# Double-size loads for the first two thirds of a load-bound kernel, and fifteen small loads among the last pieces

**The chip, the cores, the metric.** One core of a Trainium2 chip. The metric is the device time of one execution in microseconds (us). Profiled runs give a span a little shorter than the time (325.4 us for 327.0). PE, ACT, DVE, POOL and SP are the core's tensor, scalar, vector, GpSimd and sync engines; the sixteen transfer engines move data between memory and the core.

## The reference

```python
B, S, D, H = 8, 2048, 2048, 8          # x: (B, S, D) fp32, 134.2 MB; bias: (H, D // H)
x_heads = x.reshape(B, S, H, D // H).transpose(0, 2, 1, 3) + bias[None, :, None, :]
x_tiled = np.repeat(x_heads, 2, axis=2)
mx = x_tiled.max(axis=-1, keepdims=True)
lse = mx.squeeze(-1) + np.log(np.exp(x_tiled - mx).sum(axis=-1))      # (8, 8, 4096)
```

Every element of x is read once; 1 MB is written. The work is exp, a sum over 256 columns, and a logarithm.

## The kernel before

x goes through in 64 tiles of 2 MB: 128 partitions, two rows of 8 KB each. Loads are issued by SP. From tile 57 on a tile comes in two pieces of 1 MB, and tile 63 in eight smaller ones, so that the work after the last byte is short. Within a tile the bias is added, or its exp multiplied in, on PE, POOL and DVE, exp is ACT's, and DVE sums.

```python
K = 2                  # rows of x per partition in a tile
NBUF = 9               # tile buffers
STAGES = [(0, (BULK,)), (54, (MIXED,)), (57, (PROMPT_F1, PROMPT_F1)), (62, ...), (63, ...)]

xts = [sb.tile([P, K, D], F32, name=f"xt{i}") for i in range(NBUF)]

def rows_of(t):
    b, blk = divmod(t, NBLK)
    v = x[b, blk * P * K : (blk + 1) * P * K, :]
    if b < B - 1:
        return v.rearrange("(p k) d -> p k d", k=K)      # 16 KB in one piece per partition
    return v.rearrange("(k p) d -> p k d", k=K)          # tiles 56 to 63: rows of 8 KB

def load(t):
    after = last_uses[t - NBUF] if t >= NBUF else []
    for k0, k1, c0, c1 in pieces(t):
        loads[t, k0, c0] = on_x(t, nc.sync.dma_start(
            out=xts[t % NBUF][:, k0:k1, c0:c1], in_=rows_of(t)[:, k0:k1, c0:c1]), after)
...
# at the end of tile t's work
if k1 == K and t + NBUF < T:
    load(t + NBUF)
```

The softmax here doesn't subtract the row's maximum and nothing guards it: scores larger than these inputs give would overflow.

## Time and profile before

| | before |
|---|---|
| time, median (2 runs) | 326.97 us (326.91 to 327.03) |
| span of the profiled run | 325.4 us |
| read, rate over the span | 134.23 MB, 416 GB/s |
| busiest engines | POOL 290.7 us (89%), DVE 284.0 (87%) |

The transfer engines are busy throughout, and POOL and PE wait for loads (20.1 and 23.1 us in all), ACT and DVE mostly for them; the prediction shows the lines. Two views are added here. The first is the busy time of each engine in two stretches (from:to, its length, then busy time and number of instructions of PE, PE's weight loads, DVE, ACT and POOL; last come PE's granted clock, the busy share of the transfer engines and GB/s).

```profile
15.00:205.00 190.00, 158.96 (x371) 57.13 (x371) 172.96 (x78) 158.84 (x243) 176.61 (x39) 0.94 1.01 428
285.00:310.00 25.00, 23.91 (x87) 11.23 (x87) 24.66 (x120) 24.06 (x50) 19.08 (x35) 0.88 1.01 421
```

The last number of each line: 428 GB/s with 16 KB rows, 421 in the tail with 8 KB rows.

The second is the times at which the sixteen transfer engines report a load as landed. A load has landed when the last of the sixteen has reported (ACT takes up tile 62's second piece at 314.65, the sixteenth report came at 314.63). Taken from the trace (us):

```
load                        first engine   last engine   apart
tile 0                          7.61           8.51       0.90
tile 41                       208.63         210.31       1.68
tile 55                       277.14         279.52       2.38
tile 56 (first of 8 KB rows)  282.11         284.48       2.37
tile 62, second piece         311.91         314.63       2.72
last piece of tile 63         317.27         319.78       2.51
```

The engines drift apart, from 0.90 us to 2.51, and don't come together again. The last one sets when a piece can be used, and the program ends 5.6 us after its last report.

### The profile page before, as it was taken

What the parts mean: (1) busy time and instruction counts of PE and PEld (TensorE: products, weight loads), DVE (VectorE), ACT (ScalarE), POOL (GpSimd) and SP (SyncE); (2) the same over time, 40 slices, a digit from 0 to 9 for tenths busy, and PEclk for the clock granted to TensorE, in tenths of its full rate; (3) what the DMA queues carried; (4) which work ended last, traced back from release to release, by engine and by line L of the source; (5) the groups of instructions that cost most, each with busy time, mean ns of one, the idle gap of its engine ahead of it and who ended that gap; (6) DMA issues with size and microseconds to landing.
All of it is one profiled execution on the core that took longest, in us unless ns stands there. A gap on an engine that the chain in (4) does not pass through costs nothing.

```text
span 325.4 us, 2350 instructions
## 1 busy us (share of the span) xinstructions
PE 263.2 (81%) x649; PEld 98.6 (30%) x649; DVE 284.0 (87%) x306; ACT 264.7 (81%) x425; POOL 290.7 (89%) x123
## 2 busy tenths in 40 slices
PE   5398999599888789779779788887877897399984
PEld 2033333233323223223223223323223332044442
DVE  1008999999999999998998899989899799999985
ACT  1139999499969878987887969698788778889995
POOL 7999999899999999999999999999999899958874
PEclk9999999899979987997997979798998989569999
DMA  7999999999999999999999999999999999999995
GB/s 293 428 435 429 427 433 422 425 433 429 427 427 431 425 424 433 425 425 434 426 425 431 431 422 427 429 429 427 431 427 426 429 425 429 415 421 421 424 394 154
DMA packets 11934, 135.42 MB, mean 416 GB/s; under 512 B 1361, under 2 KB 1745, under 8 KB 2961
## 3 DMA queue, kind: packets, MB, share of 16 engines
q1 hardware_dynamic: 11824, 135.27, 98.9%
q8 instruction: 5, 0.08, 0.1%
q14 instruction: 7, 0.06, 0.0%
q0 software_dynamic: 96, 0.00, 0.0%
q10 hardware_dynamic: 2, 0.01, 0.0%
HBM read 134.23 MB, written 1.05 MB: 416 GB/s over the span
## 4 chain that ended last, share of the span: by engine, by line
DMA 48%; DVE 35%; POOL 6%; ACT 6%; PE 3%; issue 1%; SPq 0%; DVEq 0%
DMA xt<-in_x_dram 45%; DVE R L350 29%; ACT xt L331 5%; DVE xt L343 5%; POOL xt L325 4%; DMA b<-bparts 2%; PE pair L275 2%; DVE xt L366 2%; PE one_ps L275 1%; ACT xt L293 1%; DMA brow<-in_bias_dram 1%; POOL brest L173 1%; POOL brest L175 1%; PE pair L216 0%; POOL bparts L172 0%
## 5 line engine op out<-in xcount | busy, mean ns | idle before, releaser
L325 POOL TENSOR_TENSOR xt<-xt,b_rep 128x2048 f32<-128x2048 f32 x57 | 258.8, 4543 | 20.1 <-DMA xt<-in_x_dram 20.1
L350 DVE TENSOR_REDUCE R<-xt 128x14 f32<-128x3584 f32 (+1 forms) x56 | 214.5, 3831 | 1.9
L331 ACT ACTIVATE xt<-xt 128x2560 f32<-128x2560 f32 (+5 forms) x77 | 158.1, 2062 | 13.4 <-POOL xt L325 12.5
L275 PE MATMUL pair<-xt,ident 128*128 128x512 f32 x216 | 115.1, 660 | 0.0
L275 PE MATMUL one_ps<-xt,ident 128*128 128x512 f32 x108 | 66.7, 702 | 23.1 <-DMA xt<-in_x_dram 23.1
L293 ACT ACTIVATE xt<-pair 128x1024 f32<-128x1024 f32 x54 | 56.3, 1042 | 20.7 <-PE pair L275 19.3
L275 PEld LDWEIGHTS pair<-xt,ident 128*128 128x128 f32 x216 | 46.2, 214 | 61.5 <-issue 61.5
L343 DVE TENSOR_TENSOR xt<-xt,w_ps 128x512 f32<-128x512 f32 x54 | 36.8, 681 | 27.8 <-ACT xt L331 27.7
L286 ACT ACTIVATE xt<-one_ps 128x256 f32<-128x256 f32 x108 | 40.6, 391 | 7.9 <-PE one_ps L275 7.9
L216 PE MATMUL one_ps<-b,ones 3*128 3x512 bf16 x54 | 20.7, 383 | 18.4 <-ACT xt L286 12.4
L216 PEld LDWEIGHTS <-ones 3*128 3x128 bf16 x162 | 13.5, 92 | 70.2 <-issue 63.8
L216 PE MATMUL pair<-b,ones 3*128 3x512 bf16 x108 | 32.3, 378 | 0.0
L275 PEld LDWEIGHTS one_ps<-xt,ident 128*128 128x128 f32 x108 | 17.0, 198 | 46.4 <-DMA xt<-in_x_dram 39.6
L251 PE MATMUL pair<-xt,ident 128*128 128x512 f32 (+1 forms) x36 | 21.0, 669 | 7.2 <-DMA xt<-in_x_dram 7.1
L286 ACT ACTIVATION_READ_ACCUMULATOR xt<-one_ps 128x1 f32 x108 | 23.5, 218 | 0.0
L366 DVE CUSTOM_DVE_ANT_0 xt<-xt,w_ps 128x256 f32<-128x256 f32 x61 | 22.4, 419 | 0.0
L390 POOL TENSOR_TENSOR xt<-xt 128x128 f32<-128x128 f32 (+3 forms) x39 | 13.9, 356 | 3.1
L382 POOL TENSOR_TENSOR xt<-xt,w_sb 128x256 f32<-128x256 f32 (+1 forms) x13 | 10.1, 773 | 5.4 <-ACT xt L331 4.8
L266 PE MATMUL tpair<-ident 128*128 128x128 f32 x84 | 13.6, 300 | 0.5 <-ACT res L421 0.5
L306 ACT ACTIVATE xt<-pair 128x256 f32<-128x256 f32 x33 | 12.3, 387 | 0.0
L266 PEld LDWEIGHTS tpair<-ident 128*128 128x128 f32 x84 | 11.1, 200 | 4.1 <-issue 3.0
L366 DVE CUSTOM_DVE_ANT_0 xt<-xt,one_ps 128x256 f32<-128x256 f32 x27 | 10.6, 416 | 0.7 <-ACT xt L331 0.7
(40 smaller groups left out, 68.5 us busy)
## 6 DMA issues: line engine op xcount, KB each, us to landing
xt<-in_x_dram SPq DMA_DIRECT2D x57, 2048.0 KB, 30.8
xt<-in_x_dram SPq DMA_DIRECT2D x12, 1024.0 KB, 24.7
xt<-in_x_dram SPq DMA_DIRECT2D x4, 256.0 KB, 11.4
out_dram<-res SPq DMA_DIRECT2D x1, 896.0 KB, 6.6
xt<-in_x_dram SPq DMA_DIRECT2D x2, 384.0 KB, 16.0
xt<-in_x_dram SPq DMA_DIRECT2D x2, 128.0 KB, 6.3
out_dram<-res_last SPq DMA_DIRECT2D x1, 128.0 KB, 1.7
b<-bparts POOLq DMA_DIRECT2D x3, 1.5 KB, 6.4
```

Source lines behind the costliest of these rows:

```text
L216: nc.tensor.matmul(p, lhsT=ones3, rhs=each_row(b3, h * Dh, Dh, K), start=True, stop=False,)
L251: mm = nc.tensor.matmul(p, lhsT=ident, rhs=xts[t % NBUF][:, ka:kb, c : c + w], start=False, stop=True,)
L266: nc.tensor.matmul(tps[B % 2][:, 0], lhsT=ident, rhs=ident, start=True, stop=True)
L275: mm = nc.tensor.matmul(p, lhsT=ident, rhs=xts[t % NBUF][:, :, h * Dh : (h + 1) * Dh], start=False, stop=True,)
L286: act = nc.scalar.activation(out=xts[t % NBUF][:, k, 0:Dh], in_=got[0][:, k * Dh : (k + 1) * Dh], func=ACT.Exp, accum_out=sums[:, k, 0:1],)
L293: act = nc.scalar.activation(out=xts[t % NBUF][:, :, Dh : m["pe"] * Dh].rearrange("p k (h j) -> p h k j", j=Dh), in_=got[-1].rearrange("p ...
L325: add = nc.gpsimd.tensor_tensor(out=v, in0=v, in1=each_row(b_rep, c - G0, D - c, k1 - k0), op=ALU.add)
L331: return on_x(t, nc.scalar.activation(out=v, in_=v, func=ACT.Exp), [after])
L343: mul = nc.vector.tensor_tensor(out=f, in0=f, in1=each_row(w_ps, m["pe"] * Dh - W0, n, k1 - k0), op=ALU.mult,)
L350: red = nc.vector.tensor_reduce(out=sums[:, k0:k1, h0:H], in_=v.rearrange("p k (h j) -> p k h j", j=Dh), op=ALU.add, axis=mybir.AxisListTy ...
L366: ttr = nc.vector.tensor_tensor_reduce(out=v, in0=v, in1=w, scale=1.0, scalar=0.0, op0=ALU.mult, op1=ALU.add, accum_out=dst,)
L390: done = nc.gpsimd.tensor_tensor(out=v[:, :, 0:n], in0=v[:, :, 0:n], in1=v[:, :, n : 2 * n], op=ALU.add)
```

## The change

Intent: tiles 2 to 41 are loaded in pairs, 4 MB at a time and 32 KB in one piece per partition. Eight tile buffers (four blocks) replace nine. From tile 56 on, fifteen small loads ("sinks") stand in the queue, one in front of tile 56, one in front of each 1 MB piece of tiles 57 to 62, and two in front of the first pieces of tile 63. They bring one row each to 1, 2, ... 15 partitions; nothing reads them. The start is rearranged too: bias loads from ACT, exp of the bias partly later, and for the first five tiles the bias comes from three one-row matmuls.

```diff
 K = 2
-NBUF = 9
+KB = 4
+BLOCKS = 42
+NBUF = 8
+NEARLY = 5
...
-    xts = [sb.tile([P, K, D], F32, name=f"xt{i}") for i in range(NBUF)]
+    xbs = [sb.tile([P, KB, D], F32, name=f"xb{i}") for i in range(NBUF // TB)]
+    xts = [xb[:, k : k + K] for xb in xbs for k in range(0, KB, K)]
...
     def load(t):
+        if TB <= t < BLOCKS:
+            if t % TB == 0:
+                after = [u for i in range(TB) if t >= NBUF for u in last_uses[t + i - NBUF]]
+                ins = on_x(t, nc.sync.dma_start(
+                        out=xbs[t // TB % len(xbs)], in_=rows_of(t, TB)), after)
+                for i in range(TB):
+                    loads[t + i, 0, 0] = ins
+            return
         after = last_uses[t - NBUF] if t >= NBUF else []
         for k0, k1, c0, c1 in pieces(t):
+            if t >= T - NBLK and len(sinks) < 15:
+                k = len(sinks) + 1
+                w = 256 + 4 * k
+                sinks.append(sb.tile([k, w], F32, name=f"sink{k}"))
+                nc.sync.dma_start(out=sinks[-1], in_=x[0, 0:k, 0:w])
...  (results: KB rows per partition, Ln of 32x1024 for 64x512; the start; cut)
```

More of the change, by code (lines that the diff above doesn't have):

```diff
@@ L60 @@
     H, Dh = bias.shape
-    assert D == H * Dh and S % (P * K) == 0
+    assert D == H * Dh and S % (P * KB) == 0
     NBLK = S // (P * K)
+    NB = S // (P * KB)
+    TB = KB // K
     T = B * NBLK
     T_PROMPT = STAGES[1][0]
+    T_FACTORS = T // 2
     CPE = BULK["pe"] * Dh
@@ L84 @@
     brest = sb.tile([1, 2, CPE], F32, name="brest")
-    R = [sb.tile([P, K, H, NBLK], F32, name=f"R{b}") for b in range(B - 1)]
+    R = [sb.tile([P, KB, H, NB], F32, name=f"R{b}") for b in range(B - 1)]
     R_last = sb.tile([P, H, NBLK, K], F32, name="R_last")
-    res = sb.tile([H * NBLK, B - 1, P, K, 2], F32, name="res")
+    res = sb.tile([H * NB, B - 1, P, KB, 2], F32, name="res")
     res_last = sb.tile([P, P, 2], F32, name="res_last")
-    xts = [sb.tile([P, K, D], F32, name=f"xt{i}") for i in range(NBUF)]
+    xbs = [sb.tile([P, KB, D], F32, name=f"xb{i}") for i in range(NBUF // TB)]
+    xts = [xb[:, k : k + K] for xb in xbs for k in range(0, KB, K)]
     w_ps = pp.tile([P, W2 - W0], F32, name="w_ps")
@@ L96 @@
     ps = [p[:, c : c + MM] for p in pairs for c in (0, MM)]
-    tpair = pp.tile([P, 2, K, P], F32, name="tpair")
-    tps = [tpair[:, i] for i in range(2)]
+    tp = pp.tile([P, KB, P], F32, name="tp")
     def modes_of(t):
@@ L108, in pieces, with rows_of @@
         return [(k, k + 1, c0, c1) for k in range(K) for c0, c1 in cols[k]]
-    def rows_of(t):
-        b, blk = divmod(t, NBLK)
-        v = x[b, blk * P * K : (blk + 1) * P * K, :]
+    def rows_of(t, n=1):
+        b, at = divmod(t, NBLK)
         if b < B - 1:
-            return v.rearrange("(p k) d -> p k d", k=K)
+            blk, i = divmod(at, TB)
+            v = x[b, blk * P * KB : (blk + 1) * P * KB, :]
+            return v.rearrange("(p k) d -> p k d", k=KB)[:, i * K : (i + n) * K]
+        v = x[b, at * P * K : (at + 1) * P * K, :]
@@ L116, in rows_of @@
         return v.rearrange("(k p) d -> p k d", k=K)
-    users = [[] for _ in range(T)]
+    users = [[] for _ in xbs]
     def on_x(t, ins, after):
-        known = [u for u in users[t] if u.ins.engine != ins.ins.engine]
-        for before in range(t % NBUF, t, NBUF):
-            known += users[before]
-        for u in known:
-            if u not in after:
+        buf = users[t // TB % len(xbs)]
+        for t_u, u in buf:
+            same = u.ins.engine == ins.ins.engine
+            if u not in after and (not same or t_u % NBUF == t % NBUF and t_u < t):
@@ L128, in on_x @@
                 tc.declare_no_dep(
-                    ins.ins, u.ins, reason="waited for by those it waits for"
+                    ins.ins,
+                    u.ins,
+                    reason="another tile, or waited for by those it waits for",
                 )
-        users[t].append(ins)
+        buf.append((t, ins))
         return ins
     loads = {}
+    sinks = []
     last_uses = [[] for _ in range(T)]
     def load(t):
+        if TB <= t < BLOCKS:
+            if t % TB == 0:
+                after = [u for i in range(TB) if t >= NBUF for u in last_uses[t + i - NBUF]]
+                ins = on_x(
+                    t,
+                    nc.sync.dma_start(
+                        out=xbs[t // TB % len(xbs)], in_=rows_of(t, TB)
+                    ),
+                    after,
+                )
+                for i in range(TB):
+                    loads[t + i, 0, 0] = ins
+            return
@@ L148, in load, with reload @@
             )
+    def reload(t):
+        n = t + NBUF
+        if n < BLOCKS:
+            if n % TB == TB - 1:
+                load(n - TB + 1)
+        elif n < T:
+            load(n)
     order = tc.manual_schedule()
@@ L177 @@
     for i in range(3):
-        nc.gpsimd.dma_start(out=b3[i : i + 1, :], in_=bparts[:, i])
+        nc.scalar.dma_start(out=b3[i : i + 1, :], in_=bparts[:, i])
     def spread(dst, c0, c1):
@@ L188, with first_factors, other_factors @@
         nc.vector.tensor_copy(b_rep[:, c - G0 : c - G0 + MM], ps[i])
-    for c in range(W0, W2, MM):
-        spread(w_ps[:, c - W0 : c - W0 + MM], c, c + MM)
-    nc.scalar.activation(out=w_ps, in_=w_ps, func=ACT.Exp)
-    nc.scalar.activation(out=w_sb, in_=b_rep[:, W1 - G0 :], func=ACT.Exp)
+    w_late = w_ps[:, 0 : G0 - W0]
+    spread(w_late, W0, G0)
+    nc.scalar.activation(out=w_late, in_=w_late, func=ACT.Exp)
+    def first_factors():
+        spread(one_ps, V0, W0)
+        nc.scalar.activation(out=one_ps, in_=one_ps, func=ACT.Exp)
+    def other_factors():
+        nc.scalar.activation(
+            out=w_ps[:, G0 - W0 :], in_=b_rep[:, 0 : W2 - G0], func=ACT.Exp
+        )
+        nc.scalar.activation(out=w_sb, in_=b_rep[:, W1 - G0 :], func=ACT.Exp)
     n_ps = [0]
@@ L214, in put_bias @@
             got = [one_ps, pair[:, 0:MM], pair[:, MM : 2 * MM]]
+            parts = [(ones3, b3)]
+            if n_ps[0] <= NEARLY:
+                parts = [(ones3[0:1], bparts[:, i]) for i in range(3)]
             for h, p in enumerate(got):
-                nc.tensor.matmul(
-                    p,
-                    lhsT=ones3,
-                    rhs=each_row(b3, h * Dh, Dh, K),
-                    start=True,
-                    stop=False,
-                )
+                for i, (lhsT, b) in enumerate(parts):
+                    nc.tensor.matmul(
+                        p,
+                        lhsT=lhsT,
+                        rhs=each_row(b, h * Dh, Dh, K),
+                        start=i == 0,
+                        stop=False,
+                    )
             return got + [pair]
@@ L266, in keep_warm @@
             nc.tensor.matmul(
-                tps[B % 2][:, 0], lhsT=ident, rhs=ident, start=True, stop=True
+                tp[:, 0], lhsT=ident, rhs=ident, start=True, stop=True
             )
@@ L406, in finish @@
     def finish(b):
-        nr = H * NBLK
-        tp = tps[b % 2]
-        for k in range(K):
+        nr = H * NB
+        for k in range(KB):
             nc.tensor.transpose(
@@ L418, in finish @@
             offset=tp.offset,
-            ap=[[tp.ap[0][0], nr], [1, P], [P, K], [0, 2]],
+            ap=[[tp.ap[0][0], nr], [1, P], [P, KB], [0, 2]],
         )
@@ L425, in store @@
         nc.sync.dma_start(
-            out=out[0 : B - 1].rearrange("b h (n r) -> (h n) b r", n=NBLK),
+            out=out[0 : B - 1].rearrange("b h (n r) -> (h n) b r", n=NB),
             in_=res.rearrange("q b p k r -> q b (p k r)"),
@@ L430, in finish_last @@
     def finish_last():
-        tp = tps[(B - 1) % 2][:, 0]
+        last = tp[:, KB - 1]
         nc.tensor.transpose(
-            out=tp, in_=R_last.rearrange("p h n k -> p (h n k)"), identity=ident
+            out=last, in_=R_last.rearrange("p h n k -> p (h n k)"), identity=ident
         )
         tv = bass.AP(
-            tensor=tp.tensor, offset=tp.offset, ap=[tp.ap[0], [1, P], [0, 2]]
+            tensor=last.tensor, offset=last.offset, ap=[last.ap[0], [1, P], [0, 2]]
         )
@@ L448, in sums_of @@
         if b < B - 1:
-            return R[b][:, :, :, blk]
+            return R[b][:, blk % TB * K :, :, blk // TB]
         return R_last[:, :, blk, :].rearrange("p h k -> p k h")
@@ L471 @@
     for t in range(T):
+        if t == T_FACTORS:
+            other_factors()
         xt = xts[t % NBUF]
@@ L497 @@
                     flush(for_pool)
-            if t == T_PROMPT and c0 == 0:
-                spread(one_ps, V0, W0)
-                nc.scalar.activation(out=one_ps, in_=one_ps, func=ACT.Exp)
+            if t == T_PROMPT and (k0, c0) == (0, 0):
+                first_factors()
             h0 = max(c0 // Dh, m["pe"])
@@ L525, in pool_part @@
                     later(m, t, k0, k1, sums, add)
-                if k1 == K and t + NBUF < T:
-                    load(t + NBUF)
+                if k1 == K:
+                    reload(t)
             for_pool.append(pool_part)
```

## The prediction

Its sum: 326.97 - 1.5 (blocks) + 0.1 (results) + 0.4 (sinks) = 326.0 us. The 0.4 is the author's estimate; its count of rows (15 for one engine, one for another, none for the last) was an assumption then, and the trace of the change shows it: a sink of k rows leaves k packets and k landings, and every next sink adds one landing to those of the sink before (15 of 16 in the last). That fetches make most of the spread shows in the trace of the kernel before: it stands at 0.96 to 0.97 us from tile 2 to tile 8 and rises at loads over which a fetch falls, to 1.30 and 1.79 (fetches at 49.4 and 53.3 us), from 1.67 to 2.35 (249.6) and to 2.61 (299.4); near those at 187.6 and 188.8 it narrows from 2.01 to 1.67. The largest step is 0.68 us, near the 0.7 of the range. No trace names the engine of a fetch.

> **What bounds the kernel now.** I began with the slices of the page, to see which resource is never idle.
>
> ```profile
> span 325.4 us, 2350 instructions
> ...
> PEclk9999999899979987997997979798998989569999
> DMA  7999999999999999999999999999999999999995
> GB/s 293 428 435 429 427 433 422 425 433 429 427 427 431 425 424 433 425 425 434 426 425 431 431 422 427 429 429 427 431 427 426 429 425 429 415 421 421 424 394 154
> ```
>
> The transfer row is full from the second slice to the one before last, and the rate stays at 415 to 435 GB/s whatever the engines do. The page counts 134.23 MB read; at 428 GB/s that alone is 313.6 us of 325.4. No engine reaches that: the busiest, POOL, has 290.7 us. So loads bound it, if the engines really wait for them. The next view is POOL's timeline, one late stretch (start, duration, instruction, and in brackets its idle time and what ended it).
>
> ```profile
> 200.59 4.55 POOL L325 TENSOR_TENSOR xt<-xt,b_rep 128x2048 f32<-128x2048 f32 x1 [0.36 <-DMA xt<-in_x_dram]
> 205.49 4.53 POOL L325 TENSOR_TENSOR xt<-xt,b_rep 128x2048 f32<-128x2048 f32 x1 [0.34 <-DMA xt<-in_x_dram]
> ...
> 279.59 4.55 POOL L325 TENSOR_TENSOR xt<-xt,b_rep 128x2048 f32<-128x2048 f32 x1 [0.38 <-DMA xt<-in_x_dram]
> 284.55 4.54 POOL L325 TENSOR_TENSOR xt<-xt,b_rep 128x2048 f32<-128x2048 f32 x1 [0.41 <-DMA xt<-in_x_dram]
> ```
>
> Every tile starts when its load lands, 4.90 us after the last one, and POOL then idles 0.35 us. The pace is that of the loads. Then the chain of waits at its end, where the time of the program is decided.
>
> ```profile
> 294.48 20.15 DMA xt<-in_x_dram
> 314.63 0.02 issue
> 314.65 1.71 ACT xt L331
> 316.36 0.02 issue
> 316.38 0.42 DVE xt L366
> ...
> 321.99 0.31 PE tpair L432
> 322.30 0.02 issue
> 322.33 0.38 ACT res_last L438
> ```
>
> The last large piece lands at 314.63, exp and the DVE's weighted sums follow without a gap, and the end is 10.7 us later. The landings in the trace put the very last piece at 319.78, 5.6 us before the end; it feeds the same final transpose by ACT's last exps (to 321.7), level with the DVE. Both roads move with the loads. Last, who holds a load back: the waits of the queue that issues loads, 284 to 316 us.
>
> ```profile
> SPq L143 <- DMA xt<-in_x_dram: 30.2, 13, 4.6
> ```
>
> There a load waits for an earlier load, not for a buffer: eight completion semaphores go round, so load n waits until load n-8 has landed. In the rest of the program it waits for the DVE to free a buffer, at a time when the transfer engines have some 30 us of work queued:
>
> ```profile
> xt<-in_x_dram SPq DMA_DIRECT2D x57, 2048.0 KB, 30.8
> xt<-in_x_dram SPq DMA_DIRECT2D x12, 1024.0 KB, 24.7
> ```
>
> [...] the mean load packet of 8192 B took 314.1 ns and that of 16384 B 616.8, so 2 x 314.1 - 616.8 = 11 ns are fixed. [...]
>
> **The change, part by part.**
>
> *Blocks for tiles 2 to 41.* Forty loads of 2 MB (128 rows of 16 KB) become twenty of 4 MB (128 rows of 32 KB). Bytes stay. Per pair of tiles each engine moves 8 packets instead of 16 and one completion instead of two. I take the worth of this from landings, which include the gaps between packets: the 2 MB loads land 4.895 us apart, the six 1 MB loads from 284.48 to 299.39 land 2.485 us apart. Twice 2.485 less 4.895 is 0.075 us for 8 packets and a completion per engine. If a 32 KB row is one packet, twenty blocks save 20 x 0.075 = 1.5 us. (From the packet durations: 20 x (8 x 11.4 + 9) ns = 2.0 us. I keep 1.5.) All of it is on the path, since loads are what is waited for.
>
> *Eight buffers for nine, freed in pairs.* Does a load come too late? A block's second tile is freed about 2 x 4.55 (POOL) + 2.3 (exp) + 4.5 (DVE) = 16 us after landing, plus small waits. Three more blocks, 3 x 9.71 = 29 us, are then queued behind it. About 13 us are spare; nothing starves. The pair lands together, so its second tile begins 4.2 us late at tile 42. POOL wins back 0.34 us a tile from there, so over 12 tiles to 54 the lag is gone before the last stages. Cost: 0.
>
> *The start.* Factor work moves to the middle, three small bias loads go from POOL to ACT, and for the first five tiles the bias comes in three matmuls a bank where there was one. DVE's first tile began at 25.86 after a 17.6 us idle; by the same durations it should begin near 19. But loads were never held up by this, as the rate row shows, so it is worth 0. Extra bias matmuls, 6 x 0.38 = 2.3 us a tile, use PE's earlier start.
>
> *Results.* Seven Ln of 32x1024 for seven of 64x512: about 0.4 us more each on ACT, which has slack, except the last, at tile 57, where ACT is behind until 312.1. About 0.1 us may show.
>
> *Sinks.* Fifteen small loads between the last pieces, 120 rows of 1.0 to 1.3 KB, 0.14 MB. The trace has 1 KB packets at 47 ns and completions at 9 ns, so some 55 ns a row: engine 0 gets 15, or 0.8 us; engine 14 one; engine 15 none. The mean is 0.13 MB / 428 GB/s = 0.3 us. What counts is the engine that finishes last, since a load has landed when all sixteen have. The sixteen landings of the last piece lie between 317.27 and 319.78: 2.5 us apart, most of it since instruction fetches (5 packets of 16 KB, 7 of 8 KB in the run) each push one engine back. If the late engine has a high number the sinks are free, if it is engine 0 they cost 0.8. Unknown; I take 0.4.
>
> *Semaphores.* Sinks take every second of the eight, so a 1 MB load now waits for the fourth load before it: 4 x 2.49 = 10 us ahead in place of 20. When it is released, three loads, 7.5 us, are still queued for the late engine and about 5 us for the earliest. An issue takes 0.33 us and the first packet came 1.0 us after the first issue began. Enough; cost 0. Two issues in 2.49 us do not fill the queue either.
>
> Sum: 326.97 - 1.5 + 0.1 + 0.4 = 326.0 us.
>
> **Rivals.** First, a 32 KB row is cut into two packets of 16 KB: the gain falls to some 20 completions, 0.2 us, and the sinks stay, so 327.3. For it: no row above 16 KB exists in this trace. Against: rows of 2, 3, 8 and 16 KB all stand as one packet each. Second, halving the loads in flight starves the engines in the last 40 us: the rate falls below 420 GB/s there, and a gap of 0.5 us per piece over 15 pieces would make 333. Against: the 10 us in flight. Third, the tail becomes bound by engines: it is only just ahead, DVE idles 0.2 to 0.3 us per piece from 309 on, and ACT first waits for a load at 312.1. If lag from blocks or the longer Ln remains, the end follows DVE and the gain is cut by up to 1 us: 327. Fourth, [...] the last engine comes 0.7 us sooner or later for no reason in the diff. Fifth, the start mattered after all: DVE is busy without pause until 117 us, so its 7 us head start would count. But loads flow at the full rate all that time, so no.
>
> **Range and chances.** Gain of 1.5 to 2.0 with 32 KB packets, 0.2 without; sinks 0 to 0.8; lag 0 to 1; fetches plus or minus 0.7. Together 324.8 to 327.4 for 8 in 10. Two per cent is 6.5 us: faster by that would need the loads to exceed any rate seen, 1 in 100; slower needs starvation, 4 in 100.
>
> **What would show it.** Right: load packets of 32768 B of about 1.21 us in the trace, blocks landing 9.71 us apart, 430 to 432 GB/s in the slices from 15 to 210 us, unchanged 420 or more from 285 us to the last piece, the last piece landing about 1.1 us earlier (318.6), and the same 5.6 us after it. Sinks: the queue's waits in the last 40 us for loads of four back, with no dip in the transfer row, and the spread of the last landing changed by under 1 us. Wrong: 16384 B packets in the block stretch, a dip in the rate row from 270 us on, POOL or DVE without waits for loads at tiles 50 to 56, or a distance from last landing to end above 6.5 us.

## The result

The change measured 327.28 us (327.19 to 327.38, 2 runs) against 326.97. A ratio is the mean time of one kernel's fast runs over that of the other's of the same rounds, so it is not quite the ratio of the medians quoted; here 1.0015, interval 0.9991 to 1.0039. Repeated in five rounds (below) it was 327.41 us, ratio 1.0024 (1.0012 to 1.0036): slightly slower, where 1.0 us less had been forecast.

The page of the changed kernel, slices:

```profile
span 325.1 us, 2413 instructions
...
DMA  8999999999999999999999999999999999999995
GB/s 314 462 403 435 452 429 408 452 440 399 452 440 411 438 440 424 423 444 436 411 448 430 411 448 431 411 433 423 423 429 432 425 426 423 419 418 417 409 355 156
```

The transfer engines are as full as before. In the block stretch the slices swing more; in slices 35 to 39 of the 40 the rate falls (419, 418, 417, 409, 355, where before stood 415, 421, 421, 424, 394). The two stretches, same columns as above:

```profile
15.00:205.00 190.00, 162.25 (x391) 59.01 (x390) 171.10 (x76) 157.75 (x240) 171.62 (x39) 0.92 1.00 430
285.00:310.00 25.00, 23.86 (x90) 11.64 (x89) 24.36 (x123) 23.61 (x49) 17.75 (x37) 0.88 1.01 414
```

So 428 became 430 where blocks are loaded, and 421 became 414 where the sinks are, with no idle transfer time. POOL's timeline in the block stretch:

```profile
199.02 9.03 POOL L383 TENSOR_TENSOR xb<-xb,b_rep 128x2048 f32<-128x2048 f32 x2 [0.65 <-DMA xb<-in_x_dram]
208.75 9.04 POOL L383 TENSOR_TENSOR xb<-xb,b_rep 128x2048 f32<-128x2048 f32 x2 [0.70 <-DMA xb<-in_x_dram]
```

Pairs now come 9.73 us apart (9.71 in most of the run; twice 4.895 is 9.79), and POOL still waits for each. The chain of waits at the end:

```profile
303.32 10.97 DMA xb<-in_x_dram
314.28 0.02 issue
314.31 1.71 ACT xb L389
316.01 0.02 issue
316.03 0.42 DVE xb L424
...
321.64 0.31 PE tp L489
321.96 0.02 issue
321.98 0.38 ACT res_last L495
```

It is the same chain, 0.35 us earlier. The loads as a group (size, median time from issue to landing), and what the load queue waited for from 284 to 318 us:

```profile
xb<-in_x_dram SPq DMA_DIRECT2D x20, 4096.0 KB, 21.5
xb<-in_x_dram SPq DMA_DIRECT2D x17, 2048.0 KB, 22.8
xb<-in_x_dram SPq DMA_DIRECT2D x12, 1024.0 KB, 10.7
```

```profile
SPq L177 <- DMA xb<-in_x_dram: 21.8, 12, 2.1
```

A 1 MB piece now lands 10.7 us after its issue, where it took 24.7. Either fact, the shorter queue or the extra rows, could explain the tail.

Landings say where the time went. Tile 41's block lands at 208.68 (before 210.31: 1.63 us gained), tile 55 at 277.41 (279.52: 2.11 gained), tile 56 at 282.37 (284.48: 2.11). Then the gain melts: the second piece of tile 62 lands at 314.28 (314.63: 0.35 left). Over those twelve pieces the last engine falls from 2.04 to 3.76 us behind the first.

A sink's k rows go to k engines: in the trace of the change it leaves k packets (one of 1040 B, two of 1056 B, up to fifteen of 1264 B) and k landings, each some 0.2 us behind one of the load before it (one more report comes 0.4 to 0.9 us after its issue), and each sink adds one engine to those of the sink before. The engines are numbered here in the order in which they come in, so the landings show which one is late. In the repeat, the two-row sink lands at 281.18 and 282.72, right behind tile 56's load, whose last report is at 282.53. In a run where each sink had one row (below), the sink in that place landed at 281.27. So the first engine is 1.5 us ahead (281.18 against 282.72), and the late one is the *second*. (In the first run of the change every sink from the second on has a row 0.18 to 0.21 us behind the last landing of the load before it.) Follow its packets in the trace, back from the last landing: up to the sixth sink its 8 KB packets take 309 to 325 ns. After that one to four of every eight take 340 to 445. (The trace does not name the engine of a packet; a packet is taken to follow the one that ends where it starts, and each last landing has to fit.) No load packet in the tail of the kernel before did that, except where an instruction fetch came by: of the 8192 B packets from 280 us on, 4 took over 325 ns before, 173 in the first run of the change and 198 in its repeat.

### The profile page after: what moved, and what is told of

Same layout as the page of the kernel before. It is cut to its first block, busy times and chain, and to the rows that moved or that the text cites. A ratio compares the mean times of both kernels' runs of the same rounds, so it can differ in the third digit from the quotient of the medians.

```text
span 325.1 us, 2413 instructions
## 1 busy us (share of the span) xinstructions
PE 269.4 (83%) x691; PEld 102.6 (32%) x691; DVE 284.0 (87%) x306; ACT 266.1 (82%) x426; POOL 287.6 (88%) x120
## 4 chain that ended last, share of the span: by engine, by line
DMA 38%; PE 19%; DVE 19%; POOL 14%; ACT 10%; issue 0%; SPq 0%; DVEq 0%
DMA xb<-in_x_dram 37%; DVE R L408 14%; POOL xb L383 14%; ACT xb L389 7%; PE pair L333 6%; PE one_ps L333 3%; PE pair L274 3%; DVE xb L401 2%; PE pair L309 2%; DVE xb L424 2%; PE one_ps L274 1%; PE pair L226 1%; ACT xb L351 1%; ACT xb L364 1%; PE tp L324 1%; DMA brow<-in_bias_dram 1%
## 5 line engine op out<-in xcount | busy, mean ns | idle before, releaser
L383 POOL TENSOR_TENSOR xb<-xb,b_rep 128x2048 f32<-128x2048 f32 x57 | 257.5, 4540 | 20.6 <-DMA xb<-in_x_dram 20.6
L408 DVE TENSOR_REDUCE R<-xb 128x14 f32<-128x3584 f32 (+1 forms) x56 | 214.5, 3830 | 1.9
L389 ACT ACTIVATE xb<-xb 128x2560 f32<-128x2560 f32 (+5 forms) x77 | 157.2, 2052 | 13.0 <-POOL xb L383 11.3
L333 PE MATMUL pair<-xb,ident 128*128 128x512 f32 x216 | 113.8, 653 | 0.0
L333 PE MATMUL one_ps<-xb,ident 128*128 128x512 f32 x108 | 66.9, 705 | 11.4 <-DMA xb<-in_x_dram 11.3
L351 ACT ACTIVATE xb<-pair 128x1024 f32<-128x1024 f32 x54 | 55.5, 1027 | 22.5 <-PE pair L333 22.5
L333 PEld LDWEIGHTS pair<-xb,ident 128*128 128x128 f32 x216 | 46.0, 213 | 60.8 <-issue 60.8
L401 DVE TENSOR_TENSOR xb<-xb,w_ps 128x512 f32<-128x512 f32 x54 | 36.7, 680 | 26.2 <-ACT xb L389 26.1
L344 ACT ACTIVATE xb<-one_ps 128x256 f32<-128x256 f32 x108 | 40.0, 380 | 6.5 <-PE one_ps L333 6.4
L424 DVE CUSTOM_DVE_ANT_0 xb<-xb,w_ps 128x256 f32<-128x256 f32 x61 | 22.3, 416 | 0.0
## 6 DMA issues: line engine op xcount, KB each, us to landing
xb<-in_x_dram SPq DMA_DIRECT2D x12, 1024.0 KB, 10.7
```

Source lines behind the costliest of these rows:

```text
L333: mm = nc.tensor.matmul(p, lhsT=ident, rhs=xts[t % NBUF][:, :, h * Dh : (h + 1) * Dh], start=False, stop=True,)
L344: act = nc.scalar.activation(out=xts[t % NBUF][:, k, 0:Dh], in_=got[0][:, k * Dh : (k + 1) * Dh], func=ACT.Exp, accum_out=sums[:, k, 0:1],)
L351: act = nc.scalar.activation(out=xts[t % NBUF][:, :, Dh : m["pe"] * Dh].rearrange("p k (h j) -> p h k j", j=Dh), in_=got[-1].rearrange("p ...
L383: add = nc.gpsimd.tensor_tensor(out=v, in0=v, in1=each_row(b_rep, c - G0, D - c, k1 - k0), op=ALU.add)
L389: return on_x(t, nc.scalar.activation(out=v, in_=v, func=ACT.Exp), [after])
L401: mul = nc.vector.tensor_tensor(out=f, in0=f, in1=each_row(w_ps, m["pe"] * Dh - W0, n, k1 - k0), op=ALU.mult,)
```

## The experiments

Theory ROWS: a small row costs the engine that carries it, and also another one, depending on the partition that it is written to. Rivals: LANES, the sinks take half of the eight completion semaphores (the counters by which loads report their landing; in the traces the 77 loads of the kernel before use eight, the fifteen sinks four), so too few loads are in flight; FETCH, instruction fetches happened to fall on an engine that was late already. Each kernel ran in five rounds beside the kernel before; three groups, each on one chip, whose medians of before were 326.75 (e1 to e4), 326.76 (e5 to e8) and 326.99 (e9 to e12). All results were correct.

| run | time, us | ratio (interval) | tile 62's second piece lands | engines apart there | packets over 325 ns |
|---|---|---|---|---|---|
| e1 the change | 327.41 | 1.0024 (1.0012 to 1.0036) | 314.49 | 3.99 | 198 |
| e2 blocks only | 325.17 | 0.9954 (0.9942 to 0.9966) | 312.33 | 2.23 | 3 |
| e3 sinks only | 328.95 | 1.0091 (1.0055 to 1.0126) | 316.48 | 4.20 | 177 |
| e4 one row each | 325.26 | 0.9959 (0.9946 to 0.9972) | 312.32 | 2.20 | 3 |
| e5 eight rows, partitions 0 to 7 | 327.79 | 1.0030 (1.0017 to 1.0042) | 314.93 | 4.74 | 80 |
| e6 eight rows, 0, 4 ... 28 | 326.09 | 0.9976 (0.9964 to 0.9989) | 313.12 | 3.03 | 3 |
| e7 upper half | 326.43 | 0.9989 (0.9975 to 1.0002) | 314.09 | 3.56 | 200 |
| e8 half rows | 326.37 | 0.9991 (0.9979 to 1.0004) | 313.45 | 3.10 | 89 |
| e12 two rows, 0 and 4 | 325.85 | 0.9970 (0.9956 to 0.9983) | 312.91 | 2.74 | 3 |

In all of these the program ends 5.5 to 5.6 us after its last piece has landed, so the landings carry over to the time. (Landings are those of the profiled run; that of e7 was its slowest, 326.99 us.)

**e1, the change again.** No edit.

> The changed kernel again, as the measure for the others. Every theory: 327.3 us, ratio 1.001 to kernel before. The last 2 MB load lands some 2.1 us earlier than before, and the late engine falls from 2.1 to 3.8 us behind the first during the sinks.

As expected, with a larger spread (3.99 us).

**e2, without the sinks.**

```diff
-            if t >= T - NBLK and len(sinks) < 15:
-                ... (the small load)
```

> The change without its fifteen small loads. Theory ROWS (each small row costs the engine that carries it[...], so the late engine loses 1.8 us in the tail) and theory LANES (small loads take every second completion semaphore, so fewer loads are in flight): 325.0 us, ratio 0.994, last-piece spread about 2.1 to 2.5 us as before. Theory FETCH (instruction fetches fell on an engine that was late already): stays at 327, ratio 1.000, spread above 3 us.

325.17 us, and the spread stays at 2.2 us to the end. FETCH falls: the fetches stand at nearly the same times as in e1 (from 238 us on: 238.3, 248.2, 270.5, 298.4 and 298.4), and nothing is lost. Blocks are worth what was forecast, and the sinks 327.41 - 325.17 = 2.24 us. One thing to know of this kernel: in its chain of waits the load is gone from the tail. From 276.61 to 314.06 us the chain is ACT's own work, where in the change a load ends at 314.28. ACT and the loads are level now, so landings that come earlier still need not bring more; no run tests that.

**e3, the kernel before with the sinks.** The same five lines are put into the load function of the kernel before.

> The kernel before with the fifteen small loads alone. ROWS and LANES: 328.7 us, ratio 1.005, since the 1.8 us loss stands without the gain. FETCH: 327.0, ratio 1.000.

328.95 us, 2.2 us more than before. (One of six runs took 333.11 and widens the interval.) The loss needs nothing from the blocks.

**e4, sinks of one row.**

```diff
-                sinks.append(sb.tile([k, w], F32, name=f"sink{k}"))
-                nc.sync.dma_start(out=sinks[-1], in_=x[0, 0:k, 0:w])
+                sinks.append(sb.tile([1, w], F32, name=f"sink{k}"))
+                nc.sync.dma_start(out=sinks[-1], in_=x[0, 0:1, 0:w])
```

A sink of one row is one packet (the first sink of the change: one of 1040 B), so one engine carries it.

> The change with each of its fifteen small loads cut to one row, to partition 0: as many loads and as many semaphores taken, 15 rows instead of 120. ROWS: [...] 15 x 57 ns = 0.85 us if it is the late one, nothing else is lengthened: 325.0 to 325.9, ratio 0.994 to 0.997, 8192 B packets in the tail at 314 ns on average. LANES: 327.3 as the change, ratio 1.001.

325.26 us. LANES falls: as many loads, as many semaphores taken, and nothing lost (0.09 us over e2): the only engine that carries rows is the first, which is some 1.5 us ahead (281.18 against 282.72 in e1). What remains is the rows. Which part of them?

**e5 and e6, the same eight rows to other partitions.** The trace of the change shows where to look. From one 1 MB piece to the next the late engine takes 2.54 us with a sink of two or three rows between, 2.58, 2.58, 2.60, 2.67 and 2.70 with four to eight, and 2.67 to 2.72 with nine to twelve (before: 2.47 to 2.50 where no fetch falls). Most of the growth comes with the fifth to eighth row, which go to partitions 4 to 7. The late engine carries a row of the smaller sinks already, so these are taken to be rows of other engines. Theory PLACE: a row holds up an engine that depends on the partition it is written to, even if another carries it. These two kernels have equal rows and bytes and differ in the partitions only.

```diff
-                k = len(sinks) + 1
-                w = 256 + 4 * k
-                sinks.append(sb.tile([k, w], F32, name=f"sink{k}"))
-                nc.sync.dma_start(out=sinks[-1], in_=x[0, 0:k, 0:w])
+                k, w = 8, 288
+                sinks.append(sb.tile([P, w], F32, name=f"sink{len(sinks) + 1}"))
+                nc.sync.dma_start(out=sinks[-1][0:8], in_=x[0, 0:k, 0:w])      # e5
+                nc.sync.dma_start(out=sinks[-1][0:29:4], in_=x[0, 0:k, 0:w])   # e6
```

> All fifteen small loads have 8 rows of 1152 B, to the neighbouring partitions 0 to 7. Theory PLACE [...]: the second, late engine carries 15 rows (0.9 us)[...]: 2.3 to 2.8 us over the blocks alone, 327.5 to 328.0 us. Theory SOURCE (the rows are slow to read, wherever they go): as the next kernel. Theory OWN (a row costs only its own engine, but more than its 57 ns): 2.2 us, as the next kernel.

> The same 15 loads of 8 rows from the same place, but to partitions 0, 4, 8 ... 28[...]. PLACE: only 15 x 57 ns = 0.9 us on the late engine: 326.0 us, few 8192 B packets above 325 ns in the tail (under 30, where the change had 198). SOURCE and OWN: no different from the kernel with partitions 0 to 7, within 0.3 us.

327.79 against 326.09: 1.7 us for nothing but the partitions, and 80 lengthened packets against 3. (The step in the expectation from 0.9 us to 2.3 to 2.8 was the author's estimate for rows that others carry.) The tail stretch of e5, then of e6:

```profile
285.00:310.00 25.00, 23.56 (x87) 11.54 (x87) 24.51 (x123) 22.82 (x49) 17.75 (x36) 0.87 1.01 415
```

```profile
285.00:310.00 25.00, 24.60 (x95) 12.47 (x94) 24.88 (x125) 23.36 (x49) 17.75 (x37) 0.86 1.02 420
```

The same bytes flow at 415 and at 420 GB/s. SOURCE and OWN fall. The packets of the rows themselves took 53.4 ns on average in e5 and 51.8 in e6, so it is not the engines carrying them that lose. The late engine does: of its last 48 packets of 8 KB, 14 took over 340 ns in e5 (up to 414), and none over 318 in e6. Call rows to partitions 4 to 7 that other engines carry foreign; by the landings of the change they are the suspects. Thirteen sinks stand before the last 1 MB piece and bring 13 x 4 = 52 of them; the 8 of the two sinks behind it may be written before the late engine is through as well, by engines that are ahead (in the change the last sink's first row lands at 311.52, the piece at 314.28). Between e5 and e6 they make 314.93 - 313.12 = 1.81 us, 30 to 35 ns a row (an estimate: 1.81 us over 60 or 52 rows).

**e7, the change's rows moved up by 64 partitions.**

```diff
-                nc.sync.dma_start(out=sinks[-1], in_=x[0, 0:k, 0:w])
+                nc.sync.dma_start(out=sinks[-1][64 : 64 + k], in_=x[0, 0:k, 0:w])
```

> The change with the small loads' rows in partitions 64 to 78 in place of 0 to 14. PLACE: [...] the late one, which keeps only its own 14 rows, 0.8 us: 326.0 us[...], about 200 lengthened packets still, but on others. SOURCE and OWN: 327.4 as the change.

326.43 us, 1.0 us less than the change, with as many lengthened packets (200), but on others: the second engine's took 309 to 320 ns in the two pieces behind the seventh and eighth sink. It missed 326.0, since another engine came last. Its rows show which. In the ninth sink no row lands behind the last report of the piece before by the usual 0.17 us (300.44 after 300.39); in the tenth one does (303.23 after 303.06), and in all later ones. An engine that carries its first row in the tenth sink is the tenth. The packets of the engine that came last, followed back to the tenth sink, took up to 431 ns. So with the partitions the lengthening moved to another engine.

**e8, rows half as wide.**

```diff
-                w = 256 + 4 * k
+                w = 128 + 2 * k
```

> The change with rows half as wide (520 to 632 B). If a row costs by its bytes, own and foreign: 1.1 to 1.2 us over the blocks alone, 326.3 us. If it costs by the row whatever its size: 327.4 as the change.

326.37 us: half the bytes, half the loss (1.20 of 2.24 us over blocks only). Rows cost by their bytes.

**e12, two rows, to partitions 0 and 4.**

```diff
-                k, w = 8, 288            # as e6
-                nc.sync.dma_start(out=sinks[-1][0:29:4], in_=x[0, 0:k, 0:w])
+                k, w = 2, 288
+                nc.sync.dma_start(out=sinks[-1][0:5:4], in_=x[0, 0:k, 0:w])
```

> As the kernel with 8 rows to partitions 0, 4 ... 28, but 2 rows only, to partitions 0 and 4: 30 rows in all instead of 120. If only the rows on the late, second engine count: 326.0, no different. If the bytes or the number of rows count: a quarter of its loss, 325.4.

325.85 us, ratio 0.9970; e6 with four times the rows had 0.9976. The last 1 MB piece lands 0.58 us later than in e2, where e6's lands 0.79 later: with a quarter of the volume most of the loss remains, so it is mainly the rows on the late engine that count. For its 13 rows that is 45 ns a row.

**e9, e10 and e11, the other parts of the change**, all without sinks.

```diff
-BLOCKS = 42
+BLOCKS = 2        # e9
+BLOCKS = 56       # e10
-NEARLY = 5
+NEARLY = 0        # e11 (with BLOCKS = 42)
```

> The change without small loads and without blocks: 2 MB loads from tile 2 on, all else (eight buffers, the start, the results) as changed. If the gain of the blocks alone (325.2) is all from fewer packets, as the prediction had it: 326.8, ratio 1.000, 2 MB loads 4.89 us apart. If the start or the buffers give it: 325.2 to 325.5.

327.03 us, ratio 1.0003 (0.9990 to 1.0015). Eight buffers, the start and the results are worth nothing that shows (the interval leaves room for 0.5 us); the 1.5 us are the blocks'.

> Blocks alone, up to tile 55 in place of 41, no small loads. By packets: seven more blocks, 7 x 0.075 = 0.5 us less than with 42, 324.6. If the pair that lands together leaves POOL and DVE behind at the last stages, as the prediction feared: 325.5 to 329, and DVE busy without idle time until the end.

328.59 us, ratio 1.0051 (1.0038 to 1.0064). The last piece lands at 317.10, 0.47 us before e2's, as packets would have it. But the program ends 9.3 us after it. From 285 to 312 us, e10 and then e2:

```profile
285.00:312.00 27.00, 23.71 (x86) 11.44 (x85) 27.00 (x128) 26.40 (x55) 20.68 (x36) 0.82 1.01 416
```

```profile
285.00:312.00 27.00, 25.40 (x104) 13.28 (x103) 26.51 (x135) 26.98 (x58) 19.86 (x42) 0.93 1.01 418
```

DVE (the third busy time) has no free moment in e10; in the same time it does 128 instructions against 135. With pairs up to tile 55 the engines enter the last stages late and never catch up. POOL shows why, e10's timeline:

```profile
267.34 9.05 POOL L378 TENSOR_TENSOR xb<-xb,b_rep 128x2048 f32<-128x2048 f32 x2 [0.68 <-DMA xb<-in_x_dram]
277.05 13.55 POOL L378 TENSOR_TENSOR xb<-xb,b_rep 128x2048 f32<-128x2048 f32 x3 [0.67 <-DMA xb<-in_x_dram]
```

Three tiles follow without a wait from 277.05 on, where the kernel before had 0.4 us before each: the second of the last pair begins 4.5 us after it landed.

> Blocks alone (to tile 41, no small loads) with the bias of the first five tiles in one matmul a bank again, so PE starts late. If the start is worth nothing: 325.2, ratio 0.995. If it counts: 326 or more.

325.78 us (325.11 to 326.20), ratio 0.9963 (0.9950 to 0.9975). It agrees with e2's 0.9954 within the intervals; a loss of 0.3 us by the late start is not excluded, one of 1 us is. In its trace the last piece lands at 317.63 us, 0.06 after e2's, but the program ends 6.0 us later and not 5.5: from tile 56's landing at 282.55 on, the chain is PE's and ACT's work without a wait for a load. Whether that comes of the start was not tested.

The version that beats both kernels is e2: 325.17 us, 0.5% under the kernel before.

## Why the prediction was wrong, point by point

**What bounds the kernel: right.** Loads; the end follows the last landing by 5.6 us in both kernels.

**Blocks, 1.5 us: right.** 32 KB rows came as single packets of 1218 ns (mean), blocks 9.71 us apart. e2 and e9 differ by 0.0049 in their ratios, 1.6 us, and besides the sinks nothing else in the change is seen to move the time. The rival "two packets" is out.

**Eight buffers in pairs, 0: right**, and right about why 42: e10 shows the lag at the last stages that the prediction said twelve single tiles would win back.

**The start, 0: right within what e9 and e11 resolve.** DVE's first tile began at 21.3 us, not 19.

**Results, 0.1: not visible.** The distance from the last landing to the end is unchanged.

**Semaphores, 0: right.** Waits for loads four back are there, pieces land 10.7 us after their issue, and nothing starves: e4.

**Sinks, 0.4 us: this term failed; it measured 2.24 us.** The prediction said "some 55 ns a row: engine 0 gets 15, or 0.8 us; engine 14 one; engine 15 none" and took half of the range, with 0.8 us as the worst. (Its 0.13 MB of rows is 0.14; the 0.3 us stand.) Two things were wrong with it.

First, which engine was late was not known before the run. It was the second, which carries 14 of the 15 possible rows. Its own rows come to 12 x 60 = 0.72 us by the last 1 MB piece (from packets of some 51 ns and a 9 ns completion; e12 measured 0.58 for 13). That alone would have been within the prediction's 0 to 0.8.

Second, and larger, the sum had no term for a row that another engine carries and that holds up the late one all the same. Count the rows to partitions 4 to 7 up to the last 1 MB piece: the sinks of 5, 6 and 7 rows bring 1, 2 and 3, the six sinks of 8 to 13 rows bring 4 each, 30 in all, and 8 more of the two sinks behind may come while it still works. The loss there was 314.49 - 312.33 = 2.16 us; less 0.72 of its own leaves 1.4 us, or 38 to 48 ns a foreign row (an estimate: 1.44 us over 38 or 30 rows). The trace of e1 has it too: from the fourth sink on, the second engine's 80 packets of 8 KB took 1.3 us more than 313 ns each (the median in the tail of e2 is 312). e6 takes this part away from e5 by moving rows alone, e7 moves it to another engine, and e8 halves it. The runs give 30 to 35 and 38 to 48 ns a row. They show that it depends on the partitions written (e5 and e6) and on the bytes (e8); what ties those partitions to the late engine is not shown.

The prediction's rivals stood nowhere near this: it looked for starvation and for lag of the engines. Of its signs of being wrong one came, the dip in the rate from 270 us on (409 where 424 stood in slice 38), but not from starvation. That its range held the time was luck: the room up to 327.4 was made mainly for cut rows and lag, which did not come, and the 1.8 us by which the sinks were too low happened to fit in it.

**Open.** Why the second engine was late in all these kernels was not tested. Instruction fetches push single engines back (in the kernel before, one at 299.4 us goes with a load packet of 968 ns, and the spread grows from 2.37 to 2.61 us), but no run moved them.

## What to carry to other kernels

In this load-bound kernel the slowest of the sixteen transfer engines sets the pace (in e1 to e8 and e12 the program ends 5.5 to 5.6 us after its last report), so a small load can cost nothing (e4) or 2.2 us (e1) according to which engines carry its rows and to which partitions they go; its bytes over the total rate (here 0.3 us) say little, and one row to partition 0 was free fifteen times. Spread the rows of a small load: eight rows to every fourth partition, 0 to 28, cost 0.9 us over blocks alone, and 2.6 to the partitions 0 to 7 (e6 and e5). Whether an earlier place would be cheaper no run shows. Larger rows per partition save a fixed time per packet (11 ns from 8 to 16 KB, 13 ns from 16 to 32 KB; here 1.5 us for twenty loads), but end them early enough that the engines behind are caught up before the tail (pairs up to tile 41: 325.17 us, up to tile 55: 328.59).

## What else the traces show

- In a load of few rows, a row can hold up an engine that does not carry it, by the partition it goes to: an estimated 30 to 48 ns for 1.1 KB, 1.7 us between e5 and e6.
- The time that larger packets save also shows at 16 and 32 KB. The median packet of the change took 614 and 1215 ns, so 2 x 614 - 1215 = 13 ns; 1.5 us in the program.
- A fetch is not free here. In the kernel before, a fetch of 16 KB at 53.3 us took 1.09 us, the load packet right behind it 1.09 us instead of 0.61, that load landed 5.39 us after the one before instead of 4.89, and over it the engines' spread went from 1.30 to 1.79 us and did not close again (1.68 at 210 us).
- The engines drift apart within a program: 0.9 us at the first load and 2.5 at the last here.
